# One decoder step on one core: dense products and block sums of the mixers share one rotation of three PSUM banks

## The chip, the core and the metric

The kernel runs on one core of a Trainium2 chip. The core has a matrix engine (PE), a vector engine (DVE), a scalar engine (ACT), a general engine (POOL) and queues that issue DMA transfers (here all from SP). Products of PE land in PSUM, a memory of eight banks of 128 x 512 floats; a product can start only when the bank that it is given has been read out by DVE or ACT. The metric is the device time of one execution in microseconds (us).

## The reference

One step of a one-layer hybrid decoder on a prompt of 1024 tokens and on eight samples of 8 tokens. The layer normalises its input, projects it once (`h @ w_in`) and splits the columns over three mixers, then projects their outputs, attends to a memory of 256 tokens and ends with a SwiGLU block.

```python
z = h @ w_in                               # 1024 -> 3*512 + 2*256 + 256
z_mix = z_rkv + (z_sh - z_rkv) * mu_rkv    # token shift; r, k, v
kk = k * k_k;  kk = kk / max(norm(kk, per head), 1e-12)
k = k * (1 + (a - 1) * k_a)
step: S = S * w_t + (S @ a_t) b_t + v_t k_t ;  y_t = S @ r_t        # RWKV-7, 8 heads of 64
bonus = sum(r * k * r_k, per head) * v
...
xc = conv_b + sum(ext[j:j+L] * conv_w[j])                           # RG-LRU
gate_a = sigmoid(blockdiag(wa) xc + ba);  gate_i = sigmoid(blockdiag(wi) xc + bi)
...
x = x + concat(y_rwkv, y_lru, y_s5) @ w_out
x = x + mem_attend(rms_norm(x)) ;  x = x + swiglu(rms_norm(x))
```

The sums over a head (for the norm of `kk` and for the bonus) are taken by a product with a matrix of ones in blocks of 64. The recurrence is worked out in chunks of 64 tokens; each chunk needs the inverse of a triangular matrix, whose entries are products of `kk` with another operand (`ta`).

## The kernel before, in words

The tokens are cut in two halves (hf 0: 512 prompt tokens and the 64 sample tokens; hf 1: 512 prompt tokens). Activations lie with channels on the 128 partitions. Every dense product is done as three products of split operands (`mm3`, lines 177 to 179), so one 128-row output of 1024 inputs is a group of 24 matmuls into one bank. `win` (line 275) makes two such groups for each 128 columns of `w_in`, one for each half of the tokens in `GH`; they take their banks from `mmt()`, a pool of two. Block sums, the triangular products and the gates of the RG-LRU take theirs from `bst()`, a pool of its own with one bank. Five further banks (`smt()`, then `pct()` and `ctile()`) serve the S5 stage and the recurrence.

The stages, in the order of the code: low-rank factors and S5 (until about 260 us); `rwkv_operands(0, gr)` for gr 0 and 1; `lru(0, m)` for m 0 and 1; then the same for hf 1, mixed with the recurrence of the first half (`C0`), the inverses and the products with the memory; then the recurrence of the second half (`C1`), the output projection, attention and SwiGLU. `rwkv_operands` makes, for two blocks p of 128 channels: k by `zmix`, the square of it, its block sum (line 764); after both, the norm, and then for each p a run of DVE and ACT work that ends in `ta` and `kk`, their triangular product (line 822, for hf 0 also line 833), r by `zmix`, v by `zmix`, and the block sum of r times k, which is read out with v as a factor. `lru` makes x by `win`, a convolution by DVE, two gate products for each group of tokens (line 886), and then the second column block by `win`.

The order of the instructions on each engine isn't that of the code: a scheduler in the toolchain sorts them by their priority (the place in the code, with offsets from `pr`) and by when it reckons that their inputs are ready. A bank is given to the tiles of one tag in the order in which the code asks for them; the two tags `mm` and `bs` are independent of each other. PE runs its list strictly in order.

Of the kernel before, what the change touches and what calls it, by code (L numbers as in the profile page):

```python
# [7 lines left out]
F32 = mybir.dt.float32  # L8
# [6 lines left out]
P = 128  # L15
# [40 lines left out]
def body(tc, I, O, dbg=None):  # L56
# [4 lines left out]
    PSUM = bass.MemoryType.PSUM  # L61
    R, L_ = "right", "left"

    def pool(name, stack, side=None, space=None, bufs=1):
        kw = dict(name=name, bufs=bufs)
        if space is not None:
            kw['space'] = space
        if space != DRAM:
            kw['reuse_waits'] = "tile"
        if side is not None:  # L70
            kw['side'] = side
        return stack.enter_context(tc.tile_pool(**kw))
# [133 lines left out]
    mix, mps, sA, sB = ExitStack(), ExitStack(), ExitStack(), ExitStack()  # L206
# [8 lines left out]

    st0, lora, pss = ExitStack(), ExitStack(), ExitStack()
    psD = pool("psD", mps, space=PSUM)
    psB = pool("psB", mps, space=PSUM)
    psS = pool("psS", pss, space=PSUM)
    lp = pool("lora", lora, R)  # L220
    mp = pool("first", st0, R)

    def bst():
        return psB.tile([P, 512], F32, name="bs", tag="bs", bufs=1)

    def mmt():
        return psD.tile([P, 512], F32, name="mm", tag="mm", bufs=2)

    def smt():
        return psS.tile([P, 512], F32, name="s5", tag="s5", bufs=5)  # L230
# [7 lines left out]
    def load_x(hf, gi):  # L238

        (c0, n), (HH, HL) = NG[hf][gi], H[hf]  # L240
        c = slice(1 + c0, 1 + c0 + n)
        o = c0 + (584 if hf else 0)
        pt = bst()
        for k in range(0, 8, 4):
            x = mp.tile([P, 4, 296], F32, name="x", bufs=4)[:, :, :n]
            ld(x, I['xh'][:, k:k + 4, o:o + n])
            for i in range(4):
                act(HH[:, k + i, c], x[:, i], AF.Copy, scale=v_('norm_mix', k + i))
                stt(HL[:, k + i, c], x[:, i], v_('norm_mix', k + i), f32(HH[:, k + i, c]), OP.mult, OP.subtract)
            if hf == 0 and gi == 1:  # L250
                split(HA[:, k:k + 4, 513:585:9], LA[:, k:k + 4, 513:585:9], x[:, :, 224:296:9])
            act(x, x, AF.Square)
            if hf == 0:
                for i in range(4):
                    TE.matmul(pt[:, :n], ones, x[:, i], start=k + i == 0, stop=k + i == 7)
                continue
            tt(x[:, 0:2], x[:, 0:2], x[:, 2:4], OP.add, G)
            tt(x[:, 0], x[:, 0], x[:, 1], OP.add, G)
            TE.matmul(pt[:, :n], ones, x[:, 0], start=k == 0, stop=k == 4)
        act(RS[hf][:, c], pt[:, :n], AF.Ln, scale=1.0 / 1024.0, bias=k_rms)  # L260
# [14 lines left out]
    def win(hf, w, evac):  # L275

        wh, wl = w
        for c0, n in GH[hf]:
            pt = mmt()
            mm3(pt[:, :n], lambda k: (wh[:, k, :], wl[:, k, :]), hx(hf, c0, n), 8)  # L280
            evac(c0, n, min(n, 512 - c0), pt[:, :n], RS[hf][:, 1 + c0:1 + c0 + n])
# [479 lines left out]
    def blocksum(hf, src, use):  # L761
        for c0, n in GX[hf]:
            pt = bst()
            TE.matmul(pt[:, :n], blk, src[:, c0:c0 + n], start=True, stop=True)
            use(slice(c0, c0 + n), pt[:, :n])
# [7 lines left out]
    def rwkv_operands(hf, gr):  # L773
# [13 lines left out]
        for i in range(2):  # L787
# [27 lines left out]
            ld(ar_d[hf][:, p, :, 0, :], cv(kk))  # L815

            pt = bst()
            for c in range(8):
                for h in range(2):
# [748 lines left out]
    class Memory:  # L1568


        def load(self):
# [4 lines left out]
            for i in range(4):  # L1576
# [13 lines left out]
                self.h.append(h)  # L1590
                self.l.append(lo)
            pt = mmt()
            for i in range(2):
                TE.matmul(pt[:, :256], ones, acc[:, 256 * i:256 * i + 256], start=i == 0, stop=i == 1)
            self.rs = rs = mp.tile([P, 260], F32, name="mrs")
            act(rs[:, :256], pt[:, :256], AF.Ln, scale=1.0 / 1024.0, bias=k_rms)
            pt = mmt()
            for m in range(2):
                for i in range(2):
# [440 lines left out]
```

## Time and profile before

| | us |
|---|---|
| median of three runs (lowest, highest) | 1914.19 (1911.26, 1918.53) |
| profiled execution, whole | 1913.72 |
| its span in the trace | 1911.9 |
| PE busy in the span | 1783.5 (93%) |
| DVE busy | 1110.3 (58%) |
| ACT busy | 791.6 (41%) |
| POOL busy | 706.1 (37%) |

Matmuls are pipelined: one that lasts 0.29 us in a row may be followed by the next after 0.13 us. So the time of a group is read from how many start in a stretch, not from the length of one. The clock column (PEclk) is the share of full speed that TensorE was granted.

### The profile page before, as it was taken

How to read it: one execution, taken by the hardware profiler on the slowest of the kernel's cores; microseconds unless marked ns; L12 is line 12 of the kernel's file. 1: busy time of each engine (PE TensorE's matmuls, PEld its weight loads, DVE VectorE, ACT ScalarE, POOL GpSimd, SP SyncE). 2: the span in 40 equal slices, each digit the busy share in tenths (PEclk: the TensorE clock that was granted, in tenths of full speed). 3: DMA queues.
4: the chain of work that ended last, by engine and by line, in shares of the span. 5: the costliest groups of instructions: out<-in, count | busy, mean ns of one | idle time of the engine just before them, and what ended most of it. 6: DMA issues, size and time to landing. Idle time of an engine off the chain costs nothing.

```text
span 1911.9 us, 34508 instructions
## 1 busy us (share of the span) xinstructions
PE 1783.5 (93%) x13640; PEld 1621.8 (85%) x13640; DVE 1110.3 (58%) x2259; ACT 791.6 (41%) x1465; POOL 706.1 (37%) x523
## 2 busy tenths in 40 slices
PE   6998898989999999999998986999999999999997
PEld 6878787768877788797888976999999999999997
DVE  7764776797779454647755597533333332744435
ACT  8442443453434533434645355433333333411114
POOL 3311323344443423323231345644444443522235
PEclk9999998798998989999999997999999999999998
DMA  5136456437554752255553341322222213822102
GB/s 164 30 118 142 125 154 155 127 95 199 152 147 122 229 160 71 80 170 190 170 177 122 122 148 57 111 78 70 91 68 80 72 66 114 278 91 92 57 1 94
DMA packets 185426, 228.94 MB, mean 120 GB/s; under 512 B 78961, under 2 KB 127473, under 8 KB 184849
## 3 DMA queue, kind: packets, MB, share of 16 engines
q1 hardware_dynamic: 185264, 226.74, 39.0%
q8 instruction: 107, 1.75, 0.4%
q14 instruction: 55, 0.44, 0.1%
HBM read 170.47 MB, written 56.23 MB: 119 GB/s over the span
## 4 chain that ended last, share of the span: by engine, by line
PE 60%; DVE 11%; DMA 5%; issue 4%; POOL 2%; ACT 2%; SPq 1%; DVEq 0%; ACTq 0%; POOLq 0%
PE mm L179 17%; PE mm L177 17%; PE mm L178 17%; DVE Wu L81 1%; DVE tm L81 1%; DVE Y L78 1%; DMA AR<-ar 1%; DMA fg<-g 1%; PE pp L1052 1%; POOL wl L81 1%; DMA raw<-yr 1%; DVE h L78 1%; DVE bl L81 1%; ACT L75 1%; PE ss L1487 1%
## 5 line engine op out<-in xcount | busy, mean ns | idle before, releaser
L81 POOL TENSOR_TENSOR wl<-wr,wh 128x1024 fp32r<-128x1024 f32 x100 | 245.5, 2456 | 451.9 <-ACT wh L75 389.1
L177 PE MATMUL mm<-bh,st 128*128 128x288 f32 (+1 forms) x640 | 185.5, 292 | 5.3 <-ACT p L75 2.5
L177 PE MATMUL mm<-HH,wh 128*128 128x256 f32 (+2 forms) x576 | 180.9, 314 | 10.1 <-ACT Y L75 3.8
L179 PE MATMUL mm<-bh,st 128*128 128x288 f32 (+1 forms) x640 | 186.7, 293 | 1.5 <-POOL st L81 1.1
L178 PE MATMUL mm<-bl,st 128*128 128x288 f32 (+1 forms) x640 | 186.2, 292 | 0.0
L177 PE MATMUL mm<-bh,X 128*128 128x256 f32 (+1 forms) x592 | 170.6, 290 | 10.3 <-ACT X L75 10.3
L81 DVE TENSOR_TENSOR X<-X,mm 128x288 f32<-128x288 f32 (+2 forms) x200 | 100.5, 513 | 137.0 <-PE mm L179 136.2
L179 PE MATMUL mm<-gh,dl 128*128 128x288 f32 (+2 forms) x560 | 178.8, 320 | 0.2 <-POOL dl L81 0.2
L177 PE MATMUL mm<-gh,dh 128*128 128x288 f32 (+2 forms) x560 | 178.3, 318 | 0.0
L178 PE MATMUL mm<-gl,dh 128*128 128x288 f32 (+2 forms) x560 | 178.3, 318 | 0.0
L179 PE MATMUL mm<-HH,wl 128*128 128x256 f32 (+2 forms) x576 | 177.4, 308 | 0.0
L75 ACT ACTIVATE wh<-wr 128x1024 fp32r<-128x1024 f32 (+1 forms) x101 | 106.2, 1051 | 171.5 <-PE mm L178 96.8
L178 PE MATMUL mm<-HL,wh 128*128 128x256 f32 (+2 forms) x576 | 175.7, 305 | 0.0
L179 PE MATMUL mm<-bh,X 128*128 128x256 f32 (+1 forms) x592 | 171.0, 290 | 2.3 <-POOL X L81 2.3
L178 PE MATMUL mm<-bl,X 128*128 128x256 f32 (+1 forms) x592 | 170.8, 289 | 0.0
L81 DVE TENSOR_TENSOR gy<-gy,mm 128x256 f32<-128x256 f32 (+1 forms) x132 | 57.6, 437 | 175.6 <-PE mm L179 171.0
L177 PEld LDWEIGHTS mm<-HH,wh 128*128 128x128 f32 x576 | 115.8, 201 | 17.8 <-issue 6.7
L177 PEld LDWEIGHTS mm<-bh,st 128*128 128x128 f32 x640 | 122.3, 192 | 6.5 <-ACT p L75 2.8
L179 PEld LDWEIGHTS mm<-bh,st 128*128 128x128 f32 x640 | 122.7, 192 | 3.1 <-POOL st L81 2.8
L81 POOL TENSOR_TENSOR dl<-wr,dh 128x512 fp32r<-128x512 f32 x44 | 64.3, 1491 | 164.2 <-ACT dh L75 141.9
L178 PEld LDWEIGHTS mm<-bl,st 128*128 128x128 f32 x640 | 122.8, 192 | 0.1
L177 PEld LDWEIGHTS mm<-bh,X 128*128 128x128 f32 x592 | 112.4, 191 | 10.8 <-ACT X L75 10.8
(479 smaller groups left out, 5082.3 us busy)
## 6 DMA issues: line engine op xcount, KB each, us to landing
wr<-in_w_in SPq DMA_DIRECT2D x34, 512.0 KB, 4.0
X<-in_w_up SPq DMA_DIRECT2D x32, 512.0 KB, 3.5
wr<-in_w_down SPq DMA_DIRECT2D x22, 512.0 KB, 3.9
wr<-in_w_out SPq DMA_DIRECT2D x16, 512.0 KB, 5.3
wr<-in_wq SPq DMA_DIRECT2D x16, 512.0 KB, 3.6
kvb<-in_ck SPq DMA_DIRECT2D x32, 256.0 KB, 4.4
kvb<-in_cv SPq DMA_DIRECT2D x32, 256.0 KB, 4.2
wr<-in_wo SPq DMA_DIRECT2D x16, 512.0 KB, 3.5
```

Of the source, the lines that this page charges most:

```text
L75: return S.activation(out, in_, f, **kw)
L78: return V.scalar_tensor_tensor(out, a, s, b, op0=o0, op1=o1)
L81: return (eng or V).tensor_tensor(out, a, b, op=op)
L177: paced(TE.matmul(out, wh, xh, start=first and k == 0, stop=False, **kw))
L178: paced(TE.matmul(out, wh, xl, start=False, stop=False, **kw))
L179: paced(TE.matmul(out, wl, xh, start=False, stop=last and k == n - 1, **kw))
L1052: mi = TE.matmul(pvs[h][:, i, j], BK[o, i, j].rearrange("p a t -> p (a t)"), AR[o, i, h, j].rearrange("p a t -> p (a t)"), start=True, sto ...
L1487: TE.matmul(sc[32 * h:32 * h + 32, :256], qp[:, 2 * h + dt, :], kb[:, dt, :], start=dt == 0, stop=dt == 1)
```

## The change

The pool `psB` goes; block sums and dense products take their banks from one pool, `psD`, under one tag with three banks. The number of banks in use stays eight.

```diff
-    psB = pool("psB", mps, space=PSUM)
 ...
     def bst():
-        return psB.tile([P, 512], F32, name="bs", tag="bs", bufs=1)
+        return psD.tile([P, 512], F32, name="bs", tag="mm", bufs=3)

     def mmt():
-        return psD.tile([P, 512], F32, name="mm", tag="mm", bufs=2)
+        return psD.tile([P, 512], F32, name="mm", tag="mm", bufs=3)
```

The line numbers behind line 217 are one lower after the change, and the numbers of tiles three lower. No instruction is added or taken away on PE, DVE, POOL and SP; ACT loads one function table less. Their order changes on all engines, from the first block sum on until the first products of SwiGLU. With one tag, all 52 block-sum tiles and all products stand on PE in the order of the code; before, 48 of the 52 stood behind a product that the code asks for later.

PE in `rwkv_operands(0, 1)`, at the block sum of the first k (`rn` is its square, `mm_2941` before is the tile `mm_2938` after), before:

```order
L179 MATMUL mm_2915<-HH_125,wl_2912 128x288
L764 MATMUL bs_2695<-rn_2693,C_blk_443 128x288
L177 MATMUL mm_2915<-HH_125,wh_2911 128x288
...
L179 MATMUL mm_2941<-HH_125,wl_2912 128x296
L764 MATMUL bs_2698<-rn_2693,C_blk_443 128x288
L177 MATMUL mm_2941<-HH_125,wh_2911 128x296
```

and after:

```order
L179 MATMUL mm_2659<-HH_125,wl_2630 128x296
L763 MATMUL bs_2692<-rn_2690,C_blk_440 128x288
L763 MATMUL bs_2695<-rn_2690,C_blk_440 128x288
L177 MATMUL mm_2707<-HH_125,wh_2703 128x288
L178 MATMUL mm_2707<-HL_126,wh_2703 128x288
```

Before, the two sums stood 4.75 and 5.75 groups of products behind the k that they sum (`mm_2662`); now they stand directly behind it, with nothing between.

PE a little later, at the triangular product of that stage (`bs_2804` before, `bs_2801` after), before:

```order
L178 MATMUL mm_3219<-HL_126,wh_3189 128x296
L179 MATMUL mm_3219<-HH_125,wl_3190 128x296
L822 MATMUL bs_2804<-kk_2777,ta_2779 64x64 x16
L833 MATMUL bs_2829<-kk_2777,ta_2779 64x64 x2
L764 MATMUL bs_2973<-zz_2838,C_blk_443 128x288
L764 MATMUL bs_2976<-zz_2838,C_blk_443 128x288
L177 MATMUL mm_3300<-HH_125,wh_3296 128x288
```

and after:

```order
L179 MATMUL mm_2733<-HH_125,wl_2704 128x296
L763 MATMUL bs_2766<-rn_2764,C_blk_440 128x288
L763 MATMUL bs_2769<-rn_2764,C_blk_440 128x288
L821 MATMUL bs_2801<-kk_2774,ta_2776 64x64 x16
L832 MATMUL bs_2826<-kk_2774,ta_2776 64x64 x2
L177 MATMUL mm_2843<-HH_125,wh_2839 128x288
```

Before, 102 matmuls of products (the last quarter of `mm_3075` and the four groups up to `mm_3219`) stood between the last sum of the second norm (`bs_2772`) and the triangular product; now none does.

PE at the first triangular product of `rwkv_operands(0, 0)` (`s5` tiles belong to the S5 stage), before:

```order
L179 MATMUL mm_2518<-HH_125,wl_2489 128x296
L177 MATMUL mm_2518<-HH_125,wh_2488 128x296
L822 MATMUL bs_2247<-kk_2220,ta_2222 64x64 x16
L178 MATMUL mm_2518<-HL_126,wh_2488 128x296
L179 MATMUL mm_2518<-HH_125,wl_2489 128x296
```

and after:

```order
L695 MATMUL s5_1882<-XX_1723,cq_1084 128x137
L695 MATMUL s5_1883<-XX_1723,cq_1084 128x137
L821 MATMUL bs_2244<-kk_2217,ta_2219 64x64 x16
L832 MATMUL bs_2269<-kk_2217,ta_2219 64x64 x2
L177 MATMUL mm_2286<-HH_125,wh_2282 128x288
```

In front of it 424 matmuls of the products in `mm` tiles stood before, 288 now (17.7 and 12 groups of 24). In front of the second such product it was 548 and is 384.

## Rows read from the trace of the kernel before

**Rows 1.** Page, the chain of waits that ended last, by engine.
```profile
PE 60%; DVE 11%; DMA 5%; issue 4%; POOL 2%; ACT 2%; SPq 1%; DVEq 0%; ACTq 0%; POOLq 0%
```

**Rows 2.** Busy time by stretch: stretch, length, each engine (instructions), clock, DMA.
```profile
0.00:353.00 353.00, 300.93 (x2123) 272.24 (x2123) 235.57 (x534) 165.71 (x276) 106.01 (x88) 0.95 0.48 127
353.00:758.00 405.00, 375.65 (x3592) 317.48 (x3593) 292.42 (x604) 171.93 (x283) 160.17 (x129) 0.89 0.52 148
758.00:1912.00 1154.00, 1106.93 (x7927) 1032.06 (x7925) 582.30 (x1123) 453.97 (x907) 439.90 (x308) 0.98 0.33 108
```

**Rows 3.** The same for tiles named mm alone (PE, weight load, DVE, ACT).
```profile
353.00:758.00 405.00, 214.13 (x1286) 183.58 (x1287) 20.75 (x49) 3.46 (x6) 0.89 0.52 148
```

**Rows 4.** Busy time by stretch, three stretches of 10 us.
```profile
160.00:170.00 10.00, 10.00 (x76) 10.00 (x75) 4.98 (x8) 2.85 (x4) 6.41 (x4) 1.00 0.79 130
300.00:310.00 10.00, 4.54 (x58) 3.98 (x56) 9.90 (x12) 2.89 (x4) 3.58 (x2) 0.86 0.66 152
310.00:320.00 10.00, 6.55 (x20) 4.92 (x21) 5.21 (x12) 1.92 (x4) 3.48 (x3) 0.50 0.72 183
```

**Rows 5.** Waits of PE: line, waited for, us in all, times, longest.
```profile
PE mm L1601 <- DVE zb L81: 4.2, 1, 4.2
PE mm L177 <- DVE zb L81: 3.6, 6, 1.2
PE bs L833 <- DVE xa L81: 3.1, 1, 3.1
PE mm L177 <- DVE ext L81: 2.9, 1, 2.9
PE mm L177 <- DVE q L81: 2.8, 4, 1.4
```

**Rows 6.** Timeline of PE: start, us, operation, count, idle before and releaser.
```profile
221.16 1.07 PE L822 MATMUL bs<-kk,ta 64*64 64x64 f32 x26 [2.20 <-DVE kk L78]
...
261.84 0.79 PE L822 MATMUL bs<-kk,ta 64*64 64x64 f32 x18
304.87 1.15 PE L822 MATMUL bs<-kk,ta 64*64 64x64 f32 x32 [1.96 <-DVE kk L78]
309.17 0.48 PE L833 MATMUL bs<-kk,ta 64*64 64x64 f32 x4 [3.15 <-DVE xa L81]
...
316.11 0.58 PE L177 MATMUL mm<-HH,wh 128*128 128x288 f32 x1 [2.88 <-DVE ext L81]
```

**Rows 7.** Timeline of DVE, two k blocks: second half of k read out.
```profile
166.46 0.47 DVE L81 TENSOR_TENSOR zb<-mm,RS 128x296 f32<-128x296 f32 x1 [1.20 <-PE mm L179]
172.92 0.47 DVE L81 TENSOR_TENSOR zb<-mm,RS 128x296 f32<-128x296 f32 x1 [1.48 <-PE mm L179]
```

**Rows 8.** Timeline of ACT, the same two k blocks: their squares.
```profile
170.98 0.78 ACT L75 ACTIVATE rn<-zk,vec 128x576 f32<-128x576 f32 x1 [2.41 <-DVE zk L78]
...
175.16 0.78 ACT L75 ACTIVATE rn<-zk,vec 128x576 f32<-128x576 f32 x1 [0.78 <-DVE zk L78]
```

**Rows 9.** Timeline of DVE, from the second norm's sum to the triangular product.
```profile
289.21 0.46 DVE L85 TENSOR_SCALAR nr<-bs 128x288 f32<-128x288 f32 x1 [1.60 <-PE bs L764]
304.07 0.75 DVE L78 SCALAR_TENSOR_TENSOR kk<-kk,sg 128x576 f32<-128x576 f32 x1
```

**Rows 10.** Timeline of DVE, a block read out and mixed.
```profile
282.57 0.47 DVE L81 TENSOR_TENSOR zb<-mm,RS 128x296 f32<-128x296 f32 x1 [0.36 <-PE mm L179]
284.18 2.56 DVE L78 SCALAR_TENSOR_TENSOR zz<-zb,vec,zz 128x512 f32<-128x512 f32 x2 [0.96 <-ACT zz L75]
```

**Rows 11.** Timeline of DVE in the RG-LRU: x read out, the last convolution step.
```profile
315.88 0.38 DVE L81 TENSOR_TENSOR ext<-mm,RS 128x224 f32<-128x224 f32 x1
316.18 0.22 DVE L81 TENSOR_TENSOR exs<-mm,RS 128x64 f32<-128x64 f32 x1
...
341.20 0.28 DVE L78 SCALAR_TENSOR_TENSOR xc<-exs,vec,xc 128x64 f32<-128x64 f32 x1
```

**Rows 12.** Timeline of ACT in the RG-LRU: the first convolution step.
```profile
337.97 0.81 ACT L75 ACTIVATE xc<-ext,vec 128x512 f32<-128x512 f32 x1 [3.70 <-DVE zz L81]
```

## The prediction

> **What bounds the kernel now.** I read the chain of waits first, by engine: PE holds 60% of it, the next engine 11% [rows 1]. Then the busy time by stretch, cut where the mixers of each half end [rows 2]. In the first stretch (S5 and the first half's mixers) PE is busy for 301 of 353 us, in the second (the second half's mixers beside the first half's recurrence) for 376 of 405, in the rest for 1107 of 1154. DVE, the next, has 236 of 353 and 292 of 405. So PE is the bound throughout, and idles for 52, 29 and 47 us. The waits of PE by releaser say that few of these idle times are long: the largest of its kind is one of 4.2 us [rows 5]. The dense products run back to back where nothing disturbs them: 76 matmuls start in 10 us in the stretch from 160 us [rows 4], 0.132 us each, so a group of 24 takes 3.2 us. That is the unit of what follows.
>
> **What the change moves.** It adds no matmul and no read-out. Its only lever is PE's idle time. With two tags a block sum could stand on PE behind products that the code asks for later; with one tag banks go out in code order, so it can't. PE takes its list in order: where a sum stands directly behind the product from which DVE and ACT make its operand, PE now waits for the whole of their work, with the later products held behind it. Before, those later products filled the time. A third bank for dense products, on the other side, has little to save, since PE waits for read-outs of `mm` for few us [rows 5].
>
> **Waits added in the first half, after 262 us.** Each is read from the work on DVE and ACT between the last matmul of a product and the operand of the sum behind it.
> - k to its norm sum, with nothing between them now: from the start of the read-out of the second half of k to the end of the square, 166.46 to 171.76 = 5.3 us, and in the next block 172.92 to 175.94 = 3.0 us [rows 7, 8]. I take 4 us, for two blocks p: 8.
> - The second norm's sum to the triangular product: 102 matmuls covered it, none does now. From the read-out of the sum at 289.21+0.46 = 289.67 to the end of `kk` at 304.82: 15.2 us [rows 9]. At the low end four read-outs of later products, 0.47 us each [rows 10], aren't there to hold DVE up: 13. I take 15.
> - v, read out and mixed, as a factor of the bonus sum's read-out, in front of the next user of that bank: 282.57 to 286.74 = 4.2 us [rows 10]; the low end is 3.0 as for k. I take 4.
> - x of the RG-LRU to its gates: read-outs of 0.38+0.22 us, then from the first convolution step at 337.97 to the last one's end at 341.48 = 3.5 us [rows 11, 12], 4.1 together. I take 4, for two blocks m: 8.
>
> Together 8+15+4+8 = 35 us (30 to 39). Against it go three waits that the new order has no more reason for: 1.96 ahead of the triangular product, 3.15 ahead of line 833 and 2.88 ahead of the first product of the RG-LRU [rows 6], 8.0 us. Remains +27 (22 to 31).
>
> **Products left behind before 262 us.** While S5 fills PE in this stage, dense products are filler. At the first triangular product (221.16 us) 424 products had been done and 288 will have been: 136 matmuls or 5.7 groups, 18 us. At the second (it ends at 262.63) it is 548 against 384: 164 matmuls, 6.8 groups, 22 us (times by [rows 6]). If the times of these landmarks are held by DVE and the transfers, as I believe, PE idles in this time and the products come after it. They can't come out fully: DVE is freed of the read-outs and the mixing of some 3.4 blocks (0.47+0.47 of read-outs and 1.3 of mixing each, 2.56 us for two blocks [rows 10]), about 8 us, so the landmark may come that much earlier: 22-8 = 14 at the low end. I take 20.
>
> **The clock.** After the waits around 305 us the granted clock was 0.86, then 0.50 with 20 matmuls in 10 us [rows 4]: TensorE ran at its lower level of 1.2 GHz. With 6.55 us busy there, about 4 us of it at half speed cost 2 us against 2.4 GHz. The change makes up to six more waits of this kind in the first half: 0 to 12 us, I take 5.
>
> **The second half (353 to 758 us).** By the order, 2515 matmuls of dense products had been done at the end of the second chain of the recurrence, and 2335 will have been: 180 fewer, 7.5 groups, 24 us that go out of this stretch. The same waits come again: 4 norm sums, 2 triangular products, 4 bonus sums and 2 gates, 16+30+16+8 = 70 us. But here PE has the recurrence of the first half and the memory's products to do as well: 375.65 us in all, 214.13 of it in `mm` tiles [rows 2, 3], so 161.5 us of other work, which stands partly in front of the waiting sums. Its cost uncovered is 70, covered 0. The old idle time of the stretch, 29 us, shows that PE was rarely without something ready; I take a sixth uncovered, 12. The stretch comes out at -24+12 = -12 (-24 to +46).
>
> **After 758 us.** The 7.5 groups left over are done here, where PE is busy for 1107 of 1154 us [rows 2]: +24.
>
> **Sum.** 20+27+5-12+24 = +64. The profiled execution took 1913.72 us, which is 0.5 below the median of the runs, so it stands for them: 1978. All low ends give 14+22+0-24+24 = +36, 1950; all high ends 22+31+12+46+24 = +135, 2049.
>
> **Rivals.**
> 1. Faster. The third bank lets a sum or a product start while two others are read out, and nothing takes the place of the waits for a bank: 4.2+3.6+3.1+2.9+2.8 = 16.6 us [rows 5] go at most, 1897. It decides where the operands of a sum are ready by the time PE comes to it, that is, where DVE and ACT run ahead of PE. For it speaks that PE, not DVE, is full. Against it: 48 of 52 sums stood behind later products, and the DVE work between k and `kk` is 15 us long with nothing to cover it. Chance 7%. The Trainium skill speaks for this rival ("Perfetto Trace Analysis", Optimizing Tensor Performance): independent groups of matmuls should rotate through different banks, so that the read-out of one lies beside the next group's matmuls. By that rule more banks in the rotation give 1897; the trace agrees only so far as its waits of `mm` for read-outs show such a cost, 3.6 and 2.8 us, and the sums here aren't independent of the products in front of them.
> 2. The delay is made good. The second stretch has 29 us idle [rows 2] into which the late products fall, and all waits there are covered, so that neither the 29 us nor the 12 are paid: 64-29-12 = +23, 1937. For it: the other work of 161.5 us. Against: the code order of the banks holds just the late products back. Chance 18%.
> 3. The second half's waits stand uncovered too, since PE's list is fixed and a late operand holds all behind it: 47+5+46+24 = +122, 2036. For it: the 15 us of DVE work are the same there, and DVE is busier (292 of 405). Against: the other products stand in front. Chance 14%.
> 4. The change does nothing, because what sets the end is the sum of PE's work and its idle time is redistributed only: 1914. Against: after 758 us hardly any idle time is left to take up 24 us. Chance 4%.
>
> **How the numbers follow.** The sum's own case holds 57%, with a range of 1950 to 2010. Half a per cent (9.6 us) is about what a measurement of this kernel can tell from no change. Faster by more has rival 1, 7%; within it rival 4 and the edge of rival 2, 5%; slower the rest, 88%. The range is 1928 to 2022: it holds the likeliest case, rival 2 for the most part and the lower end of rival 3, and leaves some 2 in 10 outside.
>
> **What would show it.** In the changed profile PE should wait in the first half at line 763 for ACT's `rn` some 4 us at a time, at line 821 once about 15 us for `kk`, and at line 885 some 4 us for `xc`. The end of the first half's RG-LRU, 353 us here, should come about 47 to 52 us later, and the stretch from there to 758 in the old profile should be shorter by some 12 us, the rest longer by 24. The prediction is wrong in its mechanism if those waits are 1 us or less, or if the landmark at 353 hardly moves. It is wrong in size only, if the landmark moves and the second stretch gives it back (rival 2) or adds to it (rival 3).

## The result: 4% slower

The changed kernel takes 1990.05 us in the median against 1914.64 us of the kernel before in the same job, a ratio of 1.0396 (95% interval 1.0365 to 1.0426). One of the four executions of the changed kernel fell in a slower state (2505.91 us, granted clock 0.64) and is left out of the ratio; the other three lie between 1987.94 and 1991.58 us, with a median of 1988.52. The forecast was 1978. The profiled execution has a span of 1986.7 us in place of 1911.9, 74.8 more.

The first rows are the busy time by stretch of the changed kernel, the second those of the kernel before, cut where the recurrence of the first half starts on PE (its first product, line 1052 before) and where that of the second half ends (its last product, line 1170 before). Columns as in [rows 2].

```profile
0.00:421.30 421.30, 317.01 (x2128) 285.59 (x2128) 251.14 (x565) 178.00 (x291) 102.53 (x86) 0.88 0.41 107
421.30:872.00 450.70, 399.47 (x3952) 331.42 (x3952) 299.67 (x627) 168.32 (x292) 165.75 (x144) 0.89 0.47 136
872.00:1986.70 1114.70, 1070.69 (x7561) 1004.13 (x7561) 564.33 (x1068) 441.10 (x882) 432.85 (x294) 0.98 0.33 110
```

```profile
0.00:353.10 353.10, 300.93 (x2123) 272.24 (x2123) 235.67 (x534) 165.73 (x276) 106.11 (x88) 0.95 0.48 127
353.10:818.60 465.50, 432.89 (x4141) 367.08 (x4141) 329.22 (x677) 197.53 (x327) 178.71 (x146) 0.90 0.48 137
818.60:1911.90 1093.30, 1049.70 (x7377) 982.46 (x7377) 545.40 (x1049) 428.36 (x862) 421.25 (x290) 0.98 0.33 110
```

The first stretch is 68.2 us longer for the same work (2128 and 2123 matmul records). Of this 52.1 us are idle time of PE (421.3-317.0 = 104.3 against 52.2) and 16.1 us are PE busy longer, at a granted clock of 0.88 in place of 0.95. The second stretch is 14.8 us shorter, since 189 records fewer are done in it, and the third 21.4 us longer, since it does 184 more. 68.2-14.8+21.4 = 74.8.

What PE waited for in the first stretch of the changed kernel (line, waited for, us in all, times, longest), which answers to [rows 5]:

```profile
PE bs L763 <- ACT rn L75: 23.5, 4, 8.1
PE bs L821 <- DVE kk L78: 19.8, 2, 11.7
PE bs L885 <- DVE xc L78: 11.6, 2, 5.8
PE s L177 <- ACT wh L75: 11.5, 1, 11.5
PE bs L763 <- DVE zz L78: 8.4, 2, 5.3
```

Four of the five are sums, triangular products and gates that wait for their operand; the fourth, once at the start of the kernel, is there before the change too. The single waits in the timeline of PE, which answers to [rows 6] (idle time before and releaser in brackets; a line counts the records up to the end of the stretch that was asked, so the two sums at 291.95 us show three of their four records, which take 2.29 us as at 201.45):

```profile
201.45 2.29 PE L763 MATMUL bs<-rn,C_blk 128*128 128x288 f32 x4 [8.08 <-ACT rn L75]
221.87 1.98 PE L821 MATMUL bs<-kk,ta 64*64 64x64 f32 x32 [8.07 <-DVE kk L78]
...
260.46 0.45 PE L821 MATMUL bs<-kk,ta 64*64 64x64 f32 x8
260.74 0.28 PE L832 MATMUL bs<-kk,ta 64*64 64x64 f32 x2
291.95 1.81 PE L763 MATMUL bs<-rn,C_blk 128*128 128x288 f32 x3 [5.03 <-ACT rn L75]
307.24 1.81 PE L763 MATMUL bs<-rn,C_blk 128*128 128x288 f32 x3 [5.03 <-ACT rn L75]
321.23 1.97 PE L821 MATMUL bs<-kk,ta 64*64 64x64 f32 x32 [11.70 <-DVE kk L78]
...
342.46 1.33 PE L763 MATMUL bs<-zz,C_blk 128*128 128x288 f32 x2 [5.27 <-DVE zz L78]
379.40 1.81 PE L885 MATMUL bs<-xc,lruw 128*128 128x288 f32 x3 [5.74 <-DVE xc L78]
402.06 2.26 PE L885 MATMUL bs<-xc,lruw 128*128 128x288 f32 x4 [5.84 <-DVE xc L78]
```

The first triangular product comes at 221.87 us (221.16 before) and the second is done at 260.91 (262.63 before), so these landmarks stood still, with 384 dense matmuls done there in place of 548. Up to the second landmark PE idles for 59.5 us in place of 39.1, behind it (to the end of the stretch) for 44.8 in place of 13.1: there hardly anything hides the waits any more.

The chain of waits, by engine [rows 1], holds only a third of the span in this trace, and I don't read it further:

```profile
PE 34%; DVE 0%; ACT 0%; POOL 0%; issue 0%; DVEq 0%; ACTq 0%; POOLq 0%
```

The clock, in two stretches of 10 us around the sums of squares at 292 and 307 us, as [rows 4] shows it for one place before:

```profile
288.00:298.00 10.00, 6.05 (x23) 5.48 (x24) 3.49 (x5) 1.55 (x3) 2.34 (x1) 0.66 0.18 52
300.00:310.00 10.00, 4.50 (x21) 3.14 (x19) 4.09 (x7) 3.96 (x5) 2.35 (x1) 0.72 0.31 109
```

PE was idle for 4.0 us of the first and 5.5 of the second, and the granted clock is between its two levels (1.2 GHz would be 0.50, 2.4 GHz 1.00). It is above all the products right behind a wait that pay: PE's busy time in `bs` tiles, from 160 us to the end of the first stretch, is (before, then after)

```profile
160.00:353.10 193.10, 20.84 (x182) 0.93 0.59 140
```

```profile
160.00:421.30 261.30, 33.00 (x192) 0.82 0.46 105
```

12.2 us more for ten records more (gates that before came behind 353 us). The sums of squares show it best, all 24 records before, then the 16 of the first half after (least, median and largest duration in ns behind the count):

```profile
L764 PE MATMUL bs<-rn,C_blk x24: 403/407/593, 172.7 to 494.6; 128*128 128x288 f32 x16, 128*128 128x512 f32 x8
```

```profile
L763 PE MATMUL bs<-rn,C_blk x16: 687/687/849, 170.4 to 308.8; 128*128 128x288 f32 x16
```

### The profile page after: what moved, and what is told of

Read it like the earlier page. It is cut to its first block, busy times and chain, and to the rows that moved or that the text cites. A ratio compares the mean times of both kernels' runs of the same rounds, so it can differ in the third digit from the quotient of the medians.

```text
span 1986.7 us, 34504 instructions
## 1 busy us (share of the span) xinstructions
PE 1787.2 (90%) x13640; PEld 1621.1 (82%) x13640; DVE 1115.1 (56%) x2259; ACT 787.4 (40%) x1464; POOL 701.1 (35%) x523
## 5 line engine op out<-in xcount | busy, mean ns | idle before, releaser
L81 DVE TENSOR_TENSOR gy<-gy,mm 128x288 f32<-128x288 f32 (+1 forms) x132 | 57.5, 436 | 165.8 <-PE mm L179 165.8
L178 PEld LDWEIGHTS mm<-HL,wh 128*128 128x128 f32 x576 | 117.7, 204 | 5.6 <-issue 3.4
```

What stands on the lines that cost most here:

```text
L81: return (eng or V).tensor_tensor(out, a, b, op=op)
L178: paced(TE.matmul(out, wh, xl, start=False, stop=False, **kw))
```

## Experiments

The theory: with one tag a sum stands directly behind the product that its operand is made of, and PE, in order, waits for DVE and ACT. The rival: three banks are too few for both kinds, so products starve for a bank. Times "above before" are medians against the kernel before in the same job. With two tags in the one pool (`mm` two banks, `bs` one) the order on every engine is that of the kernel before, so the pool by itself changes nothing.

**One part of the tiles at a time.** Of the 52 tiles (24 block sums, 12 triangular products, 12 gates and 4 for the sums of the input at the start) only one kind takes `tag="mm"`, the rest `tag="bs"` with one bank. By this count the rival for the gates is 12 of 52 tiles, 1931 us, where the expectation counts 16. The second edit stands at line 762 of the changed kernel in sums_shared, at 816 and 829 in tri_shared, at 884 in gates_shared:

```diff
+    def bsx():
+        return psD.tile([P, 512], F32, name="bs", tag="mm", bufs=2)
 ...
-            pt = bst()
+            pt = bsx()
```

> Only the block sums (line 764) share the rotation of the dense products, here with two banks; triangular products, gates and the input's sums keep a bank of their own. Theory (the shared tag puts a sum directly behind the product that its operand is made of, so PE waits for DVE and ACT): the waits at the sums come back as after the change, 5 to 8 us at each of the four sums of squares of the first half and 3 to 5 us at the bonus sums, while the triangular products are behind some 4 groups of products and wait little; about 1955 us (1940 to 1970). Rival (three banks are too few for both kinds, dense products starve for a free bank): the waits at the sums are small and the cost goes with the number of tiles moved, 24 of 52, so about 1914 + 24/52 x 75 = 1949, but with PE waiting for read-outs of mm tiles, over 20 us in the first 421 us.

> Only the triangular products (lines 822 and 833) share the rotation of the dense products, with two banks; the rest keeps the bank of its own. Theory: PE waits for kk some 8 us at the first and 12 us or more at the third of them in the first half, and the dense products done at the second triangular product are 16 groups in place of 22.8; the sums of squares wait less than 3 us where products are left to stand in front of them; about 1945 us (1930 to 1960). Rival (starvation for banks): only 12 of 52 tiles move, 1914 + 12/52 x 75 = 1931, without waits for kk over 4 us.

> Only the gates of the RG-LRU (line 886) share the rotation of the dense products, with two banks. Theory: PE waits some 6 us for xc twice in the first half, and since no product behind the gates can be drawn forward, the last triangular product and sums of the first half are left with less cover: 15 us in all, about 1929 us (1918 to 1942); up to the second triangular product nothing changes against the kernel before. Rival (starvation for banks): 16 of 52 tiles move, 1914 + 16/52 x 75 = 1937, spread over both halves.

Measured: 1954.54 (42.7 above before, ratio 1.0227, 1.0199 to 1.0255), 1953.38 (41.5, 1.0220, 1.0197 to 1.0243) and 1916.63 us (4.8, 1.0033, 1.0021 to 1.0046). PE's waits in the first stretch of sums_shared (to 391.4 us), then in that of tri_shared (to 383.0):

```profile
PE bs L766 <- ACT rn L75: 23.6, 4, 8.2
PE bs L824 <- DVE kk L78: 13.8, 3, 7.2
...
PE bs L766 <- DVE zlast L758: 4.2, 1, 4.2
...
PE mm L177 <- DVE zz L81: 3.9, 2, 3.4
```

```profile
PE bs L824 <- DVE kk L78: 11.7, 1, 11.7
...
PE s L645 <- issue: 7.8, 1, 7.8
PE s L698 <- issue: 6.9, 1, 6.9
```

The sums wait for `rn` just as after the change (23.6 and 23.5 us), and products wait for a bank for 3.9 us (`zz`, a sum's read-out), not for over 20: the theory's rows. The totals of theory and rival, 1955 and 1949, lie too close together to tell them apart, so these rows decide. The triangular products behind them wait more than I expected (13.8 us), and alone they cost more than I expected, though with one long wait for `kk` in place of two. I put this to the dense products that can't be drawn past the first of them and are missing as filler in S5, where PE idles instead (lines 645 and 698, 7.8 and 6.9 us; the same lines, 643 and 696, have 5.0 and 3.5 before); no run shows it alone. The gates alone are a miss: their own waits came (9.7 us) and one of 12.1 for `kk` more,

```profile
PE bs L824 <- DVE kk L78: 16.3, 3, 12.1
...
PE bs L888 <- DVE xc L78: 9.7, 2, 5.8
```

and the first stretch ended at 380.6 us, 27 later than before; but the rest took 27 us less in the profile, so all of it was given back. Why here and not in the others isn't settled. The parts add up to 89 us, more than the 75 of the whole; that one wait covers another would explain it, but it isn't shown, and the parts have two banks in the rotation where the whole has three.

**The same rotation, another code order.** code_order keeps the three banks and one tag and changes where products stand in the code: both k first, r of the first block behind its sum of squares, v of it behind both sums, r and v of the second block ahead of its run of DVE work, and the second column block of `lru` ahead of its gates:

```diff
-            k = zmix(hf, 4 + p, "k")
-            ks_.append(k)
+            if not i:
+                ks_ += [zmix(hf, 4 + 2 * gr + j, "k") for j in range(2)]
 ...
-            r = zmix(hf, p, "z")
 ...
-            v = zmix(hf, 8 + p, "z")
```

> The changed kernel with the same one rotation of three banks, but the code asks for other products first: both k of a group before the first sum of squares, r and v of the first block before the triangular product, r and v of the second block ahead of its run of DVE work, and the second column block of the RG-LRU before its gates. Theory: what costs is which product stands in front of a sum, so the cost goes mostly away: sums of squares behind two groups (6.4 us, over their 5 us), the first triangular product of a group behind two (6.4 of some 12 to 15 us, some 8 us of wait left), the second behind four, gates behind two; first half's end some 25 to 35 us later than before in place of 68; about 1940 us (1920 to 1960). Rival (the shared rotation is too small or its read-outs collide): the banks are as many and as much used, so 1990 us, within 1%.

Measured: 1938.44 us, 26.6 above before (1.0141, 1.0117 to 1.0165), as expected: two thirds of the loss are gone with the same banks. PE no longer waits for `rn`; what is left in the first stretch is the triangular products, of which 11.3 us at one where I expected 8:

```profile
PE bs L828 <- DVE kk L78: 23.1, 3, 11.3
```

> The code order of the products as in code_order, but with two tags as before the change (mm two banks, bs one). Theory: with two tags the order of the code matters little, since products are drawn in front of the sums anyway; 1910 us (1895 to 1925), so the 26 us that code_order is above before come from the one tag. Rival (the code order itself costs, by other buffers held longer): it is slower than before as well, 1925 us or more.

Measured: 1912.85 us, 2.3 above before (1.0012, 0.9999 to 1.0025): with two tags the code order matters little, as expected. So the 26.6 us of code_order belong to the one tag.

**More banks.** four_shared gives the one tag four banks; three_one has two tags, `mm` with three banks and `bs` with one, and the same two lines behind.

```diff
-        return psD.tile([P, 512], F32, name="bs", tag="mm", bufs=3)
+        return psD.tile([P, 512], F32, name="bs", tag="mm", bufs=4)
 ...
-        return psS.tile([P, 512], F32, name="s5", tag="s5", bufs=5)
+        return psS.tile([P, 512], F32, name="s5", tag="s5", bufs=4)
-    PPB, CHB, WTBUF = 2, 3, 1
+    PPB, CHB, WTBUF = 2, 2, 1
```

> The changed kernel with four banks in the one rotation in place of three; S5 has four banks for it in place of five, and the recurrence two tiles of ch in place of three (what that costs by itself is in three_one). PE's order at the sums is the same as with three banks. Theory (waits for operands, set by the code order): no bank helps a sum whose operand isn't ready, so it is 70 to 80 us slower than three_one, about 1990 plus what the taken banks cost. Rival (too few banks in the rotation): most of the 75 us comes back, under 1940 us.

> Two tags as before the change, dense products with three banks, sums with one; S5 with four banks, ch with two. Control for four_shared, and the third bank for the products by itself. Theory: PE hardly waits for read-outs of mm, so the third bank brings under 10 us and the taken banks cost about as much: 1912 us (1900 to 1925). Rival of the prediction (a third bank takes the waits for a bank away): 1897 us.

Measured: four_shared 1965.20 us (54.6 above before, 1.0296, 1.0269 to 1.0324), three_one 1932.85 (22.3, 1.0121, 1.0100 to 1.0142), which is outside the 1900 to 1925 expected. The difference is 32 us, where I expected 70 to 80 and the rival under 10. In the first half the theory holds: the stretch ends at 416.2 us in one and at 358.8 in the other, 57 apart, and the waits of four_shared are those of three banks:

```profile
288.67 2.29 PE L763 MATMUL bs<-rn,C_blk 128*128 128x288 f32 x4 [5.04 <-ACT rn L75]
303.94 2.29 PE L763 MATMUL bs<-rn,C_blk 128*128 128x288 f32 x4 [5.04 <-ACT rn L75]
317.93 0.80 PE L821 MATMUL bs<-kk,ta 64*64 64x64 f32 x10 [11.70 <-DVE kk L78]
```

The second stretch gives 27 us back (457.7 us against 484.4), with 176 records fewer, and the third, where these are done, is only 3 us longer (1089.5 against 1086.8); the theory had none of this. A third bank for the products alone saves nothing that shows: three_one is slower, but the banks taken from S5 and `ch` are in that, so it doesn't measure that bank alone.

**Halves.** In first_half_shared and second_half_shared the sums of one half take `bsx()` (two banks, as above), by `bsx() if hf == 0 else bst()` and the reverse.

> Block sums, triangular products and gates of the first half share the rotation of the dense products (two banks); those of the second half have a bank of their own. Theory (nearly all of the cost arises in the first half, where no other work of PE stands beside the mixers): the end of the first half comes 60 to 70 us later than before the change, and the rest takes as long as before within 10 us: 1975 us (1965 to 1990). Rival (the loss is spread over both halves, since 28 of the 52 tiles lie in the first): 1910 + 28/52 x 75 = 1950 us.

> The other way round: only the second half's sums, triangular products and gates share the rotation of the dense products. Theory: the first half ends as before within 8 us; the waits at the sums of the second half, some 17 us in the profile of the changed kernel, are partly taken up: 1922 us (1912 to 1937). Rival (spread over both halves): 1910 + 24/52 x 75 = 1945 us.

Measured: 1986.43 us (76.9 above before, 1.0387, 1.0361 to 1.0413) and 1966.80 (57.3, 1.0293, 1.0257 to 1.0328). The first half alone costs as much as the whole change, and in the theory's range, though its end came 80 us later and not 60 to 70. The rival counts the tiles wrongly: 32 lie in the first half and 16 in the second, not 28 and 24, which makes it 1956 and 1933 us; both measured times are 30 us or more above it. But the second half isn't cheap with two banks, and there the theory missed. So one more run gave it three, with four for S5 and two for `ch` as in three_one:

> As second_half_shared, but with three banks in the rotation of the dense products (S5 has four, ch two, as in three_one, which is its control at 1933 us). Open is why sharing in the second half alone cost 57 us with two banks, while in the changed kernel the second half loses only some 10. Theory of the banks (in the second half a sum that holds its bank ahead of its operand stops the products that could stand before it, and a third bank lets them pass): some 10 us above three_one, 1943 us (1933 to 1953). Rival (in the changed kernel the second half's waits are relieved because it starts 68 us late, with everything else further on): the third bank changes nothing, some 55 us above three_one, 1985 us (1970 to 2000).

Measured: 1933.01 us, 20.2 above before (1.0103, 1.0070 to 1.0135), where three_one is 22.3 above before: sharing in the second half costs nothing beside it, not even the 10 us expected. A late start of the second half as the cause would have given 1985. The second stretch of second_half_shared, then of second_half_three:

```profile
354.60:849.80 495.20, 432.84 (x3922) 353.47 (x3923) 302.43 (x655) 179.89 (x305) 163.41 (x141) 0.82 0.43 125
```

```profile
362.10:826.90 464.80, 419.74 (x3997) 343.59 (x3997) 303.63 (x649) 181.69 (x307) 165.99 (x142) 0.85 0.46 132
```

With two banks it is 30 us longer for fewer matmuls: PE waits 24.7 us for operands of sums, triangular products and gates, against 14.0 with three, at a granted clock of 0.82 against 0.85. So the rival has a place: in the second half, where PE has other work, the number of banks decides, and three are enough for it. In the first half it is mainly the operands: it ends at 433.4 us with two shared banks (first_half_shared), 421.3 with three and 416.2 with four (four_shared, where S5 has one bank less), against 353.1 before.

**The clock.** filled and filled_to_fit put products of constants ahead of the late ones of the first half, into the bank that these then overwrite:

```diff
+    def fill(pt, n, k):
+        for _ in range(k):
+            TE.matmul(pt[:, :n], blk, c_('scan')[:, :n], start=True, stop=True)
 ...
+            fill(pt, n, 0 if hf or c0 else k)
             TE.matmul(pt[:, :n], blk, src[:, c0:c0 + n], start=True, stop=True)
```

> The changed kernel with idle PE filled in the first half: ahead of each first block sum and gate 12, ahead of each triangular product 20 products of constants go into the same bank, which the real product then overwrites (about 5 and 8 us each). Theory of the clock (in the first 421 us some 16 us of PE's added time is a lower granted clock after the waits, the rest the waits themselves): the granted clock there rises from 0.88 to 0.93 or more and 8 to 16 us come back, 1978 us (1970 to 1986), the waits for DVE and ACT staying. Rival (the clock is not set by these waits): clock as it was, 1990 us or more by what the constants run over.

> As filled, but the products of constants (0.49 us each, two records of 0.244 us) are as many as fit each wait that the changed kernel's profile shows in the first half: 10, 16, 10, 10 ahead of the four sums of squares, 16 and 23 ahead of the two long waits for kk, 6 and 10 ahead of two bonus sums, 11 ahead of each first gate, none elsewhere. In filled the constants ran over by some 36 us, while the real products of the first half after 160 us took 157 us of PE in place of 179. Theory of the clock: granted clock after 160 us 0.90 or more, and 10 to 18 us come back, 1975 us (1970 to 1981). Rival (the real products gain nothing that the end sees): 1986 us or more.

Measured: filled 2004.07 us (1.0487, 1.0467 to 1.0506), with a clock of 0.96 between 160 and 421 us: the clock came, but 200 products of constants took 100 us of PE for 63 us of waits, so the time was a miss. filled_to_fit: 1965.93 us (56.4 above before, 1.0286, 1.0263 to 1.0309). The changed kernel is 24 us slower than that, but the two come from different jobs; above the kernel before of its own job it has 74 (1988.52 against 1914.64), so some 18 us came back, the upper end of the 10 to 18 expected, though 1965.93 itself lies below the expected range. Its timeline and its stretch from 160 us to the end of the first half:

```profile
279.82 4.04 PE L763 MATMUL bs<-C_blk 128*128 128x288 f32 x16
284.04 1.24 PE L769 MATMUL bs<-rn,C_blk 128*128 128x288 f32 x4 [0.18 <-ACT rn L76]
291.58 5.01 PE L763 MATMUL bs<-C_blk 128*128 128x288 f32 x20
296.78 1.24 PE L769 MATMUL bs<-rn,C_blk 128*128 128x288 f32 x4 [0.19 <-ACT rn L76]
297.86 11.32 PE L763 MATMUL bs<-C_blk 128*128 128x288 f32 x46
309.73 1.15 PE L828 MATMUL bs<-kk,ta 64*64 64x64 f32 x32 [0.55 <-DVE kk L79]
```

```profile
160.00:402.30 242.30, 219.56 (x1472) 194.74 (x1470) 145.78 (x281) 85.34 (x123) 62.40 (x39) 0.96 0.48 112
```

The waits are filled with 4 to 5 and 11 us of constants, and the first half ends 19 us earlier than in the changed kernel (402.3 us against 421.3). The four records of two sums take 1.24 us together, where they took 2.29 in the changed kernel and in four_shared at the lower clock. The dense products gain as well, in `mm` tiles of the changed kernel, then of filled_to_fit:

```profile
160.00:421.30 261.30, 120.77 (x806) 116.42 (x804) 15.29 (x37) 0.82 0.46 105
```

```profile
160.00:402.30 242.30, 113.26 (x802) 108.73 (x800) 15.34 (x37) 0.00 (x0) 0.96 0.48 112
```

The constants take 63.2 us of PE's 219.6, so the rest took some 156 us, where the changed kernel had PE busy for 179.3 from 160 us to the end of its stretch. A part of what came back is not the change's: 0.96 is above the 0.93 that the kernel before was granted in its stretch.

## Why the prediction was right

The mechanism and the sign were right, and the time was 12 us low. One reading of the old profile was wrong: 353 and 758 us aren't where the mixers of each half end. 353.1 is the first product of the recurrence, and on PE the last gates of the halves come at 392 and 627 us. So the terms are measured here between landmarks of the program that both traces have, which leaves the forecast's sums as they are:

| term | forecast, us | measured, us |
|---|---|---|
| products left behind before 262 us | +20 | about +22: 164 matmuls at 0.132 us [rows 4]; PE idles 20.4 us more up to the landmark |
| waits after 262 us, less those gone | +27 | +32: 40.3 of new ones, less 8.0; PE idles 31.7 us more behind the landmark |
| the clock | +5 | about +14, the rest of the 68.2 |
| second half | -12 | -14.8 |
| after it | +24 | +21.4 |
| sum | +64 | +74.8 |

- The waits came where they were put: 5.03 and 5.03 for `rn` (forecast 4 each), 11.70 and 1.7 for `kk` (15), 5.27 for the bonus sum (4), 5.74 and 5.84 for the gates (4 each), together 40.3 against 35. `kk` stayed below even the low end of 13. From the end of the sum's read-out to the end of `kk` it is now 11.2 us, before 15.2, and 3.0 of these 4.0 us are three operations of DVE that ran shorter: the scan above all (from 298.30 us, 3.55 us long; after the change from 316.79 us, 1.36), the first product for `kk` (1.13, now 0.82) and that for `ta` (1.25, now 0.76). So it wasn't mainly the missing read-outs, to which the forecast gave its low end. Before, POOL was at work beside the scan (2.91 us from 297.72 us on), after the change it wasn't; that this is the reason isn't shown. The other waits were at the upper end of their bounds or above it.
- The mis-sized term is the clock. I had counted 2 us for a fall and six falls at most, from one place [rows 4]. PE's busy time in the first stretch rose by 16.1 us, a few of which belong to the gates moved in. Behind the landmark PE was busy for 115.6 us with 754 records, before for 77.4 with 568; at the 0.136 us of before, 754 would be 102.7, so 13 us more by this estimate. filled_to_fit shows that the clock is a cause of its own: with the waits filled the first half ends 19 us earlier.
- The second half: its waits for the operands of triangular products, gates and sums were 8.2 for `kk`, 6.4 for `xc` and 2.1 for `rn`, together 16.7, against a forecast of 12 of a possible 70. The cover that the forecast named, other work of PE, is there; second_half_shared shows that it takes a third bank to use it, which the forecast hadn't seen.
- Rival 1 (faster by the third bank) failed at its condition: the operands of the sums weren't ready. Rival 2 (the delay made good) didn't come: PE's idle time in the second stretch rose from 32.6 to 51.2 us. Rival 3 (second half uncovered) is near to what two banks give, not three.

What isn't settled: why gates_shared gave its 27 us back, and why four_shared made up so much behind the first half.

## What to carry to other kernels

A shared rotation of PSUM banks is also an order. Tiles of one tag get their banks in the order in which the code asks for them, so a small product whose operand is made from the product just ahead of it should, where the engine has no other work, have a tag of its own, or stand in the code behind as many independent products as its operand needs (here 5 us are two groups; moving them got two thirds of the loss back). Count the work that stands between producer and consumer on the in-order engine before and after, and price the clock with the wait: here it was a quarter on top of the idle time.

## What was not expected of the hardware

With waits of 5 us, one every 15 us, the granted clock was 0.66 and 0.72 in the 10 us around two of them. Against the kernel before, the dense groups hardly showed it (806 records in `mm` tiles kept PE busy for 121 us, 821 before for 124), while the sums of squares, most of them right behind a wait, took 0.687 us in the median in place of 0.407. But with the waits filled 802 records of dense products took 113 us, so they pay too. And filling those waits with products that nobody reads brought some 18 us back: an idle PE cost more than its idle time here.
